# One encoder block on one core: another plan for the mixer jobs, 512-column steps in half of the output projection, one operation fewer in the last chain

## The chip, the core and the metric

The kernel runs on one core of one Trainium2 chip, in one launch. The metric is the device time of that launch in microseconds (us); less is better. Before the change it is 907.31 us, the median of 3 runs (906.53 to 909.83).

## The reference, cut to what matters

One layer of a bidirectional encoder on 512 tokens of width 1024, all in float32:

```python
h = rmsnorm(x, norm1_w)
proj = h @ w_in                                  # 1024 -> 6176 columns
q, k, v, z, xbc, dt_f, dt_b = split(proj)
q, k = partial_rope(q), partial_rope(k)          # 16 heads of 64
attn = dilated_attention(q, k, v)                # three dilated windows, mixed by their denominators
ssm = ssm_mixer(z, xbc, dt_f, dt_b, ...)         # conv + SiLU, two scans (forward, backward), gate, group norm
x = x + concat([attn, ssm]) @ w_out              # 2048 -> 1024
h = rmsnorm(x, norm2_w)
u = dwconv_centered(h @ w_up, ...)               # 1024 -> 5632
x = x + (silu(u[:, :2816]) * u[:, 2816:]) @ w_down
return rmsnorm(x, final_norm_w)
```

## The kernel before

**Products.** Every float32 operand is split into a high and a low part, and each product is three matmuls: high by high, high by low, low by high. A weight tile arrives as `raw` by DMA; ACT copies its high part (`whi`), DVE or POOL subtracts to get the low part (`wlo`) (function `unit`). The free size of a matmul is 512 columns in most jobs, 256 in the jobs that compute v and z and in the output projection, and 128 in transposes.

**Stages.** (1) Warm-up matmuls, the normalised and transposed input `H`, and the first jobs (v0, z0, the step sizes dt). (2) The mixers: some 50 jobs. q0 to q7 and k0 to k7 are the projections of two heads each with rope, v0 to v3 the values, a0 to a7 the attention of two heads; b, c, x, z 0 to 3 are the projections of the state-space mixer with its convolution, s0 to s3 its states, o0 to o3 its output. (3) The output projection, `out_quarter` called for four quarters of 256 columns: 16 row blocks k, four token tiles t, three matmuls each. After a quarter the result is added to x, squared for the norm, transposed and split into `x2w`. (4) 44 up-projection jobs of 24 matmuls, 512 wide. (5) The down projection in two halves of 512 columns; in the second half the last k of each token tile are done tile by tile (`LAST = 4`), tile 3 in two parts of 256 columns, and each tile is normalised and stored as it ends.

**What sets the order.** `weave` takes the next step of the job with the smallest due time. The table `PLAN` gives each job a begin and an end, and the due times run evenly between them. The result is a program order; `list_schedule` then rebuilds the order of every engine with estimated durations (`cost`) and latencies (`LAG`), and that order is written into the program as dependencies. Each engine executes its list strictly in order: an instruction that waits holds up all that stand behind it on its engine.

**Two chains that matter later.** The rope of a q or k job (`rope_rows`, `prep_q`): ACT copies the job's result to `wkp`, DVE shuffles it into a second `wkp`, POOL and DVE multiply by tables (`rpt`), POOL adds, ACT copies the high part to `Q` or `K`, and DVE (or POOL) subtracts for the low part:

```python
        put("Qh", Q[0], qr)
        on("Ql").tensor_sub(lo, qr, f(Q[0]))
```

A b job (`ssm_b`): the convolution is three DVE steps on `B` with an ACT tanh before the third, and PE then transposes B into `trp`. An o job (`ssm_out`) runs per chunk a scan over 1024 elements on DVE (`D`), then sums and products on `D`.

**The last chain.** For each token tile: DVE adds the residual, ACT squares with a sum, DVE adds that sum to the earlier ones (`s3`), DVE scales and adds epsilon (`rs_m`, in `rstd`), POOL raises to the power -1/2, ACT and DVE scale the two halves, SyncE stores them.

Of the kernel before, what the change touches and what calls it, by code (L numbers as in the profile page):

```python
# [10 lines left out]
AF = mybir.ActivationFunctionType  # L11
# [3 lines left out]
SEQ = 512  # L15
DM = 1024
LAST = 4
HEAT = (5, 8)
ROUNDS = 4


PLAN = {"q0": (-60.6, 76), "b0": (-50.4, -31.8), "c1": (-32.3, 72.2), "s0": (-20.3, -2.1), "k1": (-12.3, 6),
# [292 lines left out]
def block_kernel(ctx: ExitStack, tc: tile.TileContext, log, x, w_in, w_out, w_up, w_down,  # L315
# [82 lines left out]
    def PS(tag):  # L398
        return T(tag)

    def SM(shape, tag, bufs=4):
        uid[0] += 1
        return sm.tile(list(shape), F32, name=f"{tag}_{uid[0]}", tag=tag, bufs=bufs)
# [69 lines left out]
            out += [(hi[:, j], lo[:, j]) for j in range(h)]  # L473
        return out

    def job_T(kind, w, c0, rhs, tag="acc"):

        wp = unit(kind, w[:, c0:c0 + 128].rearrange("(k p) c -> p k c", p=128), 8, 128)
        acc = PS(tag)
        n = len(rhs)  # L480
        for k, (rh, rl) in enumerate(rhs):
            hi, lo = wp[k]
            PE.matmul(acc, hi, rh, start=(k == 0), stop=False)
            PE.matmul(acc, hi, rl, start=False, stop=False)
            PE.matmul(acc, lo, rh, start=False, stop=(k == n - 1))
        return acc

    def tok_units(kind, w, c0, tags=("whi", "wlo"), cut=None):
# [565 lines left out]
        SP.dma_start(m, src[(k % 8) * 128:(k % 8 + 1) * 128, :])  # L1054
        split_mix(k, [m], tag)

    def out_quarter(qr, korder, banks):

        c0 = qr * 256
        wo = {}  # L1060
        for n, k in enumerate(korder):
            if k not in wo:
                k0 = k // 4 * 4
                for i, w in enumerate(unit("o", w_out[k0 * 128:(k0 + 4) * 128, c0:c0 + 256]
                                           .rearrange("(k p) c -> p k c", p=128), 4, 256)):
                    wo[k0 + i] = w
# [3 lines left out]
            for t in range(NQ):  # L1070
                o = banks[t // 2][:, (t % 2) * 256:(t % 2 + 1) * 256]
                ts = slice(t * 128, (t + 1) * 128)

                one = PE.matmul(o, mh[:, ts], hi, start=(n == 0 and t % 2 == 0), stop=False).ins
                if n == 0 and t % 2:
                    tc.add_manual_dep(one, opened.name, ISSUE_ORDER, reason="one start opens the bank")
                opened = one
                PE.matmul(o, mh[:, ts], lo, start=False, stop=False)
                PE.matmul(o, ml[:, ts], hi, start=False, stop=(n == 15 and t % 2 == 1))

    obanks = [("acc", "acc"), ("s", "o"), ("E", "y"), ("tr", "trp")]
    first = (0, 1, 2, 3, 8, 9, 10, 11, 4, 5, 12, 13, 6, 14, 15, 7)
    b0 = [PS(tg) for tg in obanks[0]]
    for k in out_quarter(0, first, b0):
# [10 lines left out]
    x2w = []  # L1095
    ss2 = SM([128, 16], "ss2", 1)
    for qr in range(4):
        hf = qr // 2
        if qr == 0:
            banks = b0  # L1100
        else:
            banks = [PS(tg) for tg in obanks[qr]]
            for k in out_quarter(qr, (12, 13, 14, 15, 5, 6, 7, 4, 0, 1, 2, 3, 8, 9, 10, 11), banks):
                if k not in parts:
                    load_mix(k, "hl2")
        cs = slice((qr % 2) * 256, (qr % 2 + 1) * 256)
        for t in range(NQ):
            if qr % 2 == 0:
# [3 lines left out]
            DVE.tensor_add(xx, xx, banks[t // 2][:, (t % 2) * 256:(t % 2 + 1) * 256])  # L1112
            scr = T("fk")
            ACT.activation(scr[:, 0:256], xx, AF.Square, accum_out=ss2[:, 4 * t + qr:4 * t + qr + 1])
        for k in (2 * qr, 2 * qr + 1):
            b = PS("acc" if qr < 3 else ("E", "y")[k % 2])
# [5 lines left out]
            x2w.append((hh, hl))  # L1122
    s2 = SM([128, 4], "s2", 1)
    DVE.tensor_reduce(s2, ss2.rearrange("p (t e) -> p t e", e=4), axis=mybir.AxisListType.X, op=ALU.add)
    r2 = rstd(s2, DM)
    b = PS("o")
    for t in range(NQ):
# [9 lines left out]
    ptags = ["acc", "s", "acc", "tr"]  # L1137

    def up_job(i, j):
        acc = job_T("u", w_up, i * 128, x2w, tag=ptags[j % 4])  # L1140
        u = T("fk")
        DVE.tensor_mul(u, acc, r2b)
        y = T("fk")
        ident_act(y, u, scale=col(P_FW, 3 * i + 1), bias=col(P_FB, i))
        DVE.scalar_tensor_tensor(y[:, 1:512], u[:, 0:511], col(P_FW, 3 * i), y[:, 1:512],
                                 op0=ALU.mult, op1=ALU.add)
        DVE.scalar_tensor_tensor(y[:, 0:511], u[:, 1:512], col(P_FW, 3 * i + 2), y[:, 0:511],
                                 op0=ALU.mult, op1=ALU.add)
        return y
# [12 lines left out]
    fw = [T("fk") for _ in range(2)]  # L1162
    ss3 = SM([128, 16], "ss3", 1)
    nss = [0] * NQ
    for hf in range(2):
        SP.dma_start(fw[hf], bass.AP(tensor=fnorm.tensor, offset=fnorm.offset + hf * 512,
                                          ap=[[0, 128], [1, 512]]))
    for hf in range(2):
# [13 lines left out]
        for k, t, cs in order:  # L1182
            gh, gl = gT[k]
            hi, lo = wd[k]
            ts = slice(t * 128, (t + 1) * 128)
            o = bank[t, cs.start][:, 0:cs.stop - cs.start]
            PE.matmul(o, gh[:, ts], hi[:, cs], start=(k == 0), stop=False)
            PE.matmul(o, gh[:, ts], lo[:, cs], start=False, stop=False)
            PE.matmul(o, gl[:, ts], hi[:, cs], start=False, stop=(k == 21))
            if k < 21:  # L1190
                continue
            n = nss[t]
            nss[t] += 1
            xx = x2[t][hf][:, cs]
            DVE.tensor_add(xx, xx, o)
            scr = T("fk")
            ACT.activation(scr[:, cs], xx, AF.Square, accum_out=ss3[:, 4 * t + n:4 * t + n + 1])
            if hf == 0:
                on("fx").tensor_mul(xx, xx, fw[0])
                continue  # L1200
            if cs.stop < 512:
                DVE.tensor_add(ss3[:, 4 * t:4 * t + 1], ss3[:, 4 * t:4 * t + 1], ss3[:, 4 * t + n:4 * t + n + 1])
                continue
            s3 = SM([128, 1], "s3", 4)
            DVE.tensor_add(s3, ss3[:, 4 * t:4 * t + 1], ss3[:, 4 * t + n:4 * t + n + 1])
# [75 lines left out]
```

## Time and profile before

| | |
|---|---|
| median of 3 runs | 907.31 us |
| the profiled execution: its own time | 908.54 us |
| its span, first to last instruction | 906.8 us |
| mean granted TensorE clock | 0.995 |
| busy PE (matmul) | 887.8 us, 98% |
| busy PEld (weight load, beside PE) | 777.1 us, 86% |
| busy DVE | 613.3 us, 68% |
| busy ACT | 467.2 us, 52% |
| busy POOL | 209.2 us, 23% |

Time in the profile is counted from the first instruction. The profiled execution took 1.74 us more than its span, and 1.23 us more than the median of the runs. All four engines run at once; the share of an engine is an average over stages. Line 142 stands for every instruction, since all are issued through one helper, so groups are told apart by the names of their tiles. The mixers reach from about 60 to 475 us, the output projection from about 440 to 540 us beside their end, the up projection to 780, the down projection to 900, and the rest is the last chain.

### The profile page before, as it was taken

What the parts mean: (1) busy time and instruction counts of PE and PEld (TensorE: products, weight loads), DVE (VectorE), ACT (ScalarE), POOL (GpSimd) and SP (SyncE); (2) the same over time, 40 slices, a digit from 0 to 9 for tenths busy, and PEclk for the clock granted to TensorE, in tenths of its full rate; (3) what the DMA queues carried; (4) which work ended last, traced back from release to release, by engine and by line L of the source; (5) the groups of instructions that cost most, each with busy time, mean ns of one, the idle gap of its engine ahead of it and who ended that gap; (6) DMA issues with size and microseconds to landing.
All of it is one profiled execution on the core that took longest, in us unless ns stands there. A gap on an engine that the chain in (4) does not pass through costs nothing.

```text
span 906.8 us, 13520 instructions
## 1 busy us (share of the span) xinstructions
PE 887.8 (98%) x5084; PEld 777.1 (86%) x5084; DVE 613.3 (68%) x1042; ACT 467.2 (52%) x971; POOL 209.2 (23%) x187
## 2 busy tenths in 40 slices
PE   8989999999999999998999999999999999999997
PEld 7968888999799889997899998888888888888886
DVE  5764879975998787888732337777777777623323
ACT  6454578656575765667843434444444444322222
POOL 1063543422542541364244210000000000000000
PEclk9999999999999999999999999999999999999999
DMA  8465332542444643226474324333333333332312
GB/s 257 140 149 138 89 99 93 163 123 70 113 121 117 173 118 99 70 82 200 132 227 157 94 71 116 94 93 93 98 107 98 93 105 105 96 108 75 116 48 93
DMA packets 123986, 105.07 MB, mean 116 GB/s; under 512 B 5776, under 2 KB 101904, under 8 KB 123920
## 3 DMA queue, kind: packets, MB, share of 16 engines
q1 hardware_dynamic: 123920, 104.20, 39.5%
q8 instruction: 40, 0.66, 0.3%
q14 instruction: 26, 0.21, 0.1%
HBM read 88.91 MB, written 5.83 MB: 104 GB/s over the span
## 4 chain that ended last, share of the span: by engine, by line
PE 88%; DVE 4%; POOL 3%; issue 2%; DMA 1%; ACT 1%; SPq 0%; POOLq 0%; ACTq 0%; DVEq 0%
PE acc L142 44%; PE tr L142 13%; PE s L142 12%; PE o L142 6%; PE y L142 5%; PE E L142 4%; PE trp L142 3%; POOL wkp L142 1%; DVE D L142 1%; POOL wlo L142 1%; DMA raw<-in_w_in_dram 1%; DMA mx<-mixA_d 1%; POOL yy L142 0%; DVE wkp L142 0%; DVE yy L142 0%
## 5 line engine op out<-in xcount | busy, mean ns | idle before, releaser
L142 ACT ACTIVATE whi<-raw 128x512 fp32r<-128x512 f32 x256 | 159.8, 630 | 266.0 <-PE acc L142 135.6
L142 DVE TENSOR_TENSOR wlo<-raw,whi 128x512 fp32r<-128x512 f32 x196 | 140.8, 722 | 99.7 <-ACT whi L142 98.7
L142 PE MATMUL acc<-H,whi 128*128 128x512 f32 x512 | 169.9, 403 | 0.0
L142 POOL TENSOR_TENSOR rs_r<-rs_m,half 128x1 f32<-128x1 f32 (+1 forms) x25 | 16.6, 665 | 425.2 <-DVE rs_m L142 425.2
L142 POOL TENSOR_TENSOR wlo<-raw,whi 128x512 fp32r<-128x512 f32 x60 | 81.4, 1362 | 141.8 <-ACT whi L142 123.6
L142 PEld LDWEIGHTS acc<-H,whi 128*128 128x128 f32 x512 | 94.7, 189 | 17.4
L142 PE MATMUL acc<-x2w,whi 128*128 128x512 f32 x352 | 109.1, 390 | 0.0
L142 PE MATMUL acc<-H,wlo 128*128 128x512 f32 x256 | 102.0, 399 | 0.0
L142 PE MATMUL acc<-whi,H 128*128 128x256 f32 x448 | 87.8, 288 | 2.2 <-ACT H L142 1.8
L142 PEld LDWEIGHTS acc<-x2w,whi 128*128 128x128 f32 x352 | 66.0, 188 | 13.6
L142 DVE SCALAR_TENSOR_TENSOR fk<-fk,prm,fk 128x511 f32<-128x511 f32 x88 | 66.1, 751 | 14.1 <-ACT fk L142 12.6
L142 PEld LDWEIGHTS acc<-whi,H 128*128 128x128 f32 x448 | 72.2, 192 | 3.5 <-ACT H L142 2.1
L142 PE MATMUL acc<-x2w,wlo 128*128 128x512 f32 x176 | 68.6, 390 | 0.0
L142 PE MATMUL acc<-wlo,H 128*128 128x256 f32 x224 | 64.6, 288 | 0.0
L142 DVE TENSOR_TENSOR PT<-tr,PT 128x512 fp32r<-128x512 f32 x64 | 43.7, 683 | 20.7 <-ACT PT L142 20.3
L142 PEld LDWEIGHTS acc<-H,wlo 128*128 128x128 f32 x256 | 48.4, 189 | 9.0
L142 PE MATMUL o<-PT,V 128*128 128x256 f32 x256 | 54.5, 296 | 0.9 <-DVE rs_m L142 0.5
L142 ACT ACTIVATE PT<-tr 128x512 fp32r<-128x512 f32 x64 | 38.1, 596 | 33.0 <-PE tr L142 32.5
L142 PE MATMUL s<-x2w,whi 128*128 128x512 f32 x176 | 54.2, 389 | 0.0
L142 PE MATMUL tr<-x2w,whi 128*128 128x512 f32 x176 | 54.2, 389 | 0.0
L142 DVE CUSTOM_DVE_ANT_0 P<-s,lmx 128x512 f32<-128x512 f32 x64 | 43.8, 684 | 13.7 <-PE s L142 11.4
L142 ACT ACTIVATE P<-P,mn 128x512 f32<-128x512 f32 x64 | 46.0, 718 | 13.0 <-DVE mn L142 12.6
(265 smaller groups left out, 2002.7 us busy)
## 6 DMA issues: line engine op xcount, KB each, us to landing
raw<-in_w_in_dram SPq DMA_DIRECT2D x48, 512.0 KB, 3.9
raw<-in_w_up_dram SPq DMA_DIRECT2D x44, 512.0 KB, 3.7
raw<-in_w_down_dram SPq DMA_DIRECT2D x22, 512.0 KB, 3.6
A<-step_d SPq DMA_DIRECT2D x16, 512.0 KB, 5.4
raw<-in_w_out_dram SPq DMA_DIRECT2D x16, 512.0 KB, 3.4
K<-K SPq DMA_DIRECT2D x48, 128.0 KB, 2.5
mx<-mixA_d SPq DMA_DIRECT2D x13, 256.0 KB, 3.5
mx<-mixS_d SPq DMA_DIRECT2D x10, 256.0 KB, 2.6
```

Source lines behind the costliest of these rows:

```text
L142: r = fn(*args, **kw)
```

## The change

It has three parts. The table `PLAN` gets new numbers, and so every engine gets a new order. The output projection has three parts instead of four quarters: columns 0 to 255, then columns 512 to 1023 at a free size of 512 with one PSUM bank per token tile (`s`, `o`, `E`, `y`), its last two k done tile by tile (`LAST_OUT = 2`), then columns 256 to 511; the up jobs take their k in the order 0, 1, 4, 5, 6, 7, 2, 3. In the last chain the earlier sums are scaled ahead (`sofar`), and one operation (`m3`) takes the place of two.

```diff
+LAST_OUT = 2
...
-PLAN = {"q0": (-60.6, 76), "b0": (-50.4, -31.8), "c1": (-32.3, 72.2), "s0": (-20.3, -2.1), "k1": (-12.3, 6),
...
+PLAN = {"b0": (-82.3, -47.8), "q0": (-78.6, 44.6), "s0": (-32, 26.5), "c1": (-23.8, 67.5), "q2": (-21, 75.6),
...
-    def out_quarter(qr, korder, banks):
+    def out_part(c0, w, korder, banks, last=0):
...
+            for t in range(NQ):
+                if n < 16 - last:
+                    out_step(t, u, w, banks, [k], wo, n == 0, n == 15)
+        for t in range(NQ if last else 0):
+            out_step(t, u, w, banks, korder[16 - last:], wo, False, True)
...
-    obanks = [("acc", "acc"), ("s", "o"), ("E", "y"), ("tr", "trp")]
...
-    for qr in range(4):
...
+    for n, (c0, w, tags, ttags) in enumerate(((0, 256, (), "acc"), (512, 512, ("s", "o", "E", "y"), "acc"),
+                                              (256, 256, ("tr", "trp"), ("E", "y")))):
...
-        acc = job_T("u", w_up, i * 128, x2w, tag=ptags[j % 4])
+        acc = job_T("u", w_up, i * 128, x2w, tag=ptags[j % 4], ks=(0, 1, 4, 5, 6, 7, 2, 3))
...
+            if hf and cs.stop == 512:
+                sofar[t] = SM([128, 1], "sofar", 4)
+                DVE.tensor_scalar(sofar[t], ss3[:, 4 * t:4 * t + 1], 1.0 / DM, EPS, op0=ALU.mult, op1=ALU.add)
...
-            s3 = SM([128, 1], "s3", 4)
-            DVE.tensor_add(s3, ss3[:, 4 * t:4 * t + 1], ss3[:, 4 * t + n:4 * t + n + 1])
-            r3 = rstd(s3, DM)
+
+            s3 = sofar[t]
+            m3, r3 = SM([128, 1], "m3", 4), SM([128, 1], "r3", 4)
+            DVE.scalar_tensor_tensor(m3, ss3[:, 4 * t + n:4 * t + n + 1], 1.0 / DM, s3, op0=ALU.mult, op1=ALU.add)
+            POOL.tensor_tensor(r3, m3, half[:, 0:1], ALU.pow)
```

The counts that follow from it: matmuls of 256 columns 1972 before and 1588 now, of 512 columns 2443 and 2635; POOL 178 tensor operations and 289 DMAs in both.

Place one, the first state-space outputs: DVE's order, before. `wkp_665` is the last step of q0's rope, `B_706` the convolution of b0, `D` the two 1024-element scans of o0's first chunks.

```order
L142 STREAM_SHUFFLE wkp_658<-acc_631 128x512
L142 TENSOR_TENSOR wkp_658<-wkp_658,rpt 128x512
L142 SCALAR_TENSOR_TENSOR D_1353<-A_1352,D_1353 128x1024
L142 TENSOR_TENSOR wkp_665<-wkp_656,Q_663 128x512
L142 SCALAR_TENSOR_TENSOR B_706<-acc_681,hcw,B_706 128x511
L142 TENSOR_TENSOR D_1353<-D_1353 128x512
L142 SCALAR_TENSOR_TENSOR B_706<-acc_681,hcw,B_706 128x511
L142 SCALAR_TENSOR_TENSOR D_1399<-A_1398,D_1399 128x1024
L142 SCALAR_TENSOR_TENSOR B_706<-acc_681,B_706 128x512
```

The same place of DVE now, where b0 is `B_656` and q0's last step is `wkp_713`:

```order
L142 SCALAR_TENSOR_TENSOR B_656<-acc_631,hcw,B_656 128x511 x2
L142 SCALAR_TENSOR_TENSOR B_656<-acc_631,B_656 128x512
L142 SCALAR_TENSOR_TENSOR D_1299<-A_1298,D_1299 128x1024
L142 STREAM_SHUFFLE wkp_706<-acc_679 128x512
L142 TENSOR_TENSOR D_1299<-D_1299 128x512
L142 TENSOR_TENSOR wkp_706<-wkp_706,rpt 128x512
L142 SCALAR_TENSOR_TENSOR D_1345<-A_1344,D_1345 128x1024
L142 TENSOR_TENSOR D_1345<-D_1345 128x512
L142 TENSOR_TENSOR wkp_713<-wkp_704,Q_711 128x512
```

The b0 job now comes before q0, so its three steps stand ahead of both scans and of q0's rope. On PE, the transposes of B moved as well; a piece of the difference (`trp_712` before, `trp_662` now; the matmuls `s` are a0's first):

```order
 L142 MATMUL acc_729<-H_103,wlo_726 128x512
-L142 MATMUL trp_712<-ident,B_706 128x128 x4
 L142 MATMUL acc_783<-H_101,whi_775 128x512
...
 L142 MATMUL acc_906<-H_103,wlo_903 128x512
-L142 MATMUL s_940<-K_761,Q_663 128x512
-L142 MATMUL s_940<-K_762,Q_663 128x512
-L142 MATMUL trp_981<-ident,xs_890 128x128
+L142 MATMUL s_983<-K_761,Q_711 128x512
+L142 MATMUL s_983<-K_762,Q_711 128x512
+L142 MATMUL trp_662<-ident,B_656 128x128 x4
 L142 MATMUL acc_1076<-H_101,whi_1068 128x512
```

Before, the transposes stood behind the first job after b0's own (job k1, `acc_729`); now they stand four jobs later.

Place two, near the end of the mixers: DVE's order, before. `wkp_4695` is the last rope step of job q7, `P` and `mn` the softmax of a6 and a7, `yy` and `rs_m` the gate and norm of o3.

```order
L142 ISA mn_4771 128x1
L142 TENSOR_TENSOR yy_4733<-yy_4733,zs_4121 128x256
L142 TENSOR_TENSOR wkp_4695<-wkp_4686,Q_4693 128x512
L142 TENSOR_TENSOR D_5172<-D_5172,CM_4136 128x512
L142 TENSOR_TENSOR wlo_5228<-raw_5221,whi_5227 128x512
L142 TENSOR_SCALAR rs_m_4742<-ssS_4740 128x1
L142 ISA P_4803,mn_4804<-s_4800,lmx 128x512
```

The same place of DVE now (q7's last rope step is `wkp_4553`):

```order
L142 TENSOR_TENSOR m_4203<-wkp_4506,o_4387 64x512
L142 TENSOR_TENSOR V_4637<-acc_4579,V_4637 128x2x64
L142 TENSOR_TENSOR wkp_4553<-wkp_4544,Q_4551 128x512
L142 ISA P_4770,mn_4771<-s_4767,lmx 128x512
L142 ISA mn_4771 128x1
L142 TENSOR_SCALAR yy_4452<-yy_4452,rs_r_4463 128x256
L142 TENSOR_TENSOR wk_4731<-E_4728,ein 128x512
L142 TENSOR_TENSOR m_4203<-m_4203,tr_4750 128x512
L142 ISA P_4803,mn_4804<-s_4800,lmx 128x512
```

q7's last rope step stood between the softmax rows `mn_4771` and `P_4803`; it now stands ahead of `P_4770`, and the v3 job's rows (`V`) have come into this place.

Place three, the end: ACT's order, before. `x_1365` and `x_1270` are the two halves of token tile 2, `x_1367` and `x_1272` those of tile 3; `fk, ss` is a square with its sum.

```order
L142 ACTIVATE fk_9250,ss_1810_8405<-x_1365_6157 128x512
L142 ACTIVATE fk_9275,ss_1810_8405<-x_1367_6162 128x256
L142 ACTIVATE x_1270_5567<-x_1270_5567,rs_r_9256 128x512
L142 ACTIVATE fk_9291,ss_1810_8405<-x_1367_6162 128x256
L142 ACTIVATE x_1272_5572<-x_1272_5572,rs_r_9297 128x512
```

The end of ACT's order now (tile 2 is `x_1355`, tile 3 `x_1357`):

```order
L142 ACTIVATE fk_9071,ss_1806_8201<-x_1357_5940 128x256
L142 ACTIVATE fk_9048,ss_1806_8201<-x_1355_5935 128x512
L142 ACTIVATE x_1270_5567<-x_1270_5567,r_1941_9051 128x512
L142 ACTIVATE fk_9089,ss_1806_8201<-x_1357_5940 128x256
L142 ACTIVATE x_1272_5572<-x_1272_5572,r_1946_9092 128x512
```

Tile 3's first square now comes before tile 2's. On PE the last 512-wide matmuls of tile 2 were followed by 24 matmuls of 256 columns; now 18 of 256 columns follow them.

## Rows read from the trace of the kernel before

**Rows 1.** Stretch 396 to 480 us: length, busy PE, PEld, DVE, ACT, POOL, clock, DMA, GB/s.

```profile
396.00:480.00 84.00, 79.56 (x569) 72.57 (x568) 58.08 (x112) 56.87 (x128) 38.09 (x31) 1.00 0.54 168
```

**Rows 2.** Chain that ended last: start us, us, engine and tile, count; three widths.

```profile
478.45 0.72 PE o L142 x6
...
542.44 0.44 PE o L142 x4
...
545.41 5.44 PE s L142 x24
```

**Rows 3.** PE's waits, 0:66, 66:396 and 396:480 us: total us, times, longest.

```profile
PE trp L142 <- DVE B L142: 3.5, 1, 3.5
...
PE y L142 <- DVE xd L142: 0.6, 1, 0.6
...
PE tr L142 <- DVE PT L142: 1.3, 2, 0.8
PE tr L142 <- ACT wkp L142: 0.7, 1, 0.7
PE o L142 <- DVE rs_m L142: 0.5, 1, 0.5
...
PE o L142 <- ACT PT L142: 0.4, 1, 0.4
PE s L142 <- DVE mn L142: 0.3, 1, 0.3
```

**Rows 4.** Timeline of DVE, 58 to 66 us; in brackets idle before, releaser.

```profile
58.45 1.10 DVE L142 TENSOR_TENSOR wkp<-wkp,Q 128x512 fp32r<-128x512 f32 x1 [1.79 <-ACT Q L142]
...
61.18 0.74 DVE L142 SCALAR_TENSOR_TENSOR B<-acc,hcw,B 128x511 f32<-128x511 f32 x1
61.84 2.70 DVE L142 TENSOR_TENSOR_SCAN D<-A,D 128x1024 f32<-128x1024 f32 x1
64.46 0.66 DVE L142 SCALAR_TENSOR_TENSOR B<-acc,B 128x512 f32<-128x512 f32 x1
...
65.68 1.70 DVE L142 TENSOR_TENSOR D<-D 128x512 f32<-128x512 f32 x1
```

**Rows 5.** Timelines of POOL, ACT and DVE, 402 to 412 us: q7's rope.

```profile
402.50 4.68 POOL L142 TENSOR_TENSOR wlo<-raw,whi 128x512 fp32r<-128x512 f32 x3
407.14 1.30 POOL L142 TENSOR_TENSOR wkp<-wkp,rpt 128x512 f32<-128x512 f32 x1
...
409.90 0.63 ACT L142 ACTIVATE Q<-wkp 128x512 fp32r<-128x512 f32 x1 [3.73 <-POOL wkp L142]
...
410.56 0.69 DVE L142 TENSOR_TENSOR wkp<-wkp,Q 128x512 fp32r<-128x512 f32 x1 [1.84 <-ACT Q L142]
411.17 0.69 DVE L142 TENSOR_TENSOR D<-D,CM 128x512 f32<-128x512 f32 x1
```

**Rows 6.** Stretch 412.44 to 432.12 us, columns as in rows 1.

```profile
412.44:432.12 19.68, 17.53 (x122) 14.79 (x121) 17.57 (x40) 15.54 (x37) 9.29 (x9) 1.00 0.68 200
```

**Rows 7.** Timelines of DVE and ACT, 897 to 902 us: the last chain.

```profile
897.40 0.69 DVE L142 TENSOR_TENSOR x<-x,tr 128x512 f32<-128x512 f32 x1 [0.46 <-PE tr L142]
...
900.27 0.42 DVE L142 TENSOR_TENSOR x<-x,acc 128x256 f32<-128x256 f32 x1 [0.76 <-PE acc L142]
...
901.34 0.15 DVE L142 TENSOR_TENSOR s<-ss 128x1 f32<-128x1 f32 x1
901.53 0.15 DVE L142 TENSOR_SCALAR rs_m<-s 128x1 f32<-128x1 f32 x1
...
900.18 0.72 ACT L142 ACTIVATE x<-x,rs_r 128x512 f32<-128x512 f32 x1 [0.38 <-POOL rs_r L142]
900.81 0.40 ACT L142 ACTIVATE fk<-x 128x256 f32<-128x256 f32 x1
```

**Rows 8.** Timeline of ACT, 9 to 11 us: the first weights.

```profile
9.85 1.15 ACT L142 ACTIVATE whi<-raw 128x512 fp32r<-128x512 f32 x2 [0.64 <-DMA raw<-in_w_in_dram]
```

More of the change, by code (lines that the diff above doesn't have):

```diff
@@ L474, in unit, with job_T @@
         return out
-    def job_T(kind, w, c0, rhs, tag="acc"):
+    def job_T(kind, w, c0, rhs, tag="acc", ks=range(KO)):
         wp = unit(kind, w[:, c0:c0 + 128].rearrange("(k p) c -> p k c", p=128), 8, 128)
         acc = PS(tag)
-        n = len(rhs)
-        for k, (rh, rl) in enumerate(rhs):
+        for k in ks:
+            rh, rl = rhs[k]
             hi, lo = wp[k]
-            PE.matmul(acc, hi, rh, start=(k == 0), stop=False)
+            PE.matmul(acc, hi, rh, start=(k == ks[0]), stop=False)
             PE.matmul(acc, hi, rl, start=False, stop=False)
-            PE.matmul(acc, lo, rh, start=False, stop=(k == n - 1))
+            PE.matmul(acc, lo, rh, start=False, stop=(k == ks[-1]))
         return acc
@@ L1055, in load_mix @@
         split_mix(k, [m], tag)
-    def out_quarter(qr, korder, banks):
-        c0 = qr * 256
+    def out_part(c0, w, korder, banks, last=0):
         wo = {}
+        u = 512 // w
         for n, k in enumerate(korder):
             if k not in wo:
[L1063 to L1066, printed above, removed]
+                k0 = k // (2 * u) * (2 * u)
+                for i, wk in enumerate(unit("o", w_out[k0 * 128:(k0 + 2 * u) * 128, c0:c0 + w]
+                                            .rearrange("(k p) c -> p k c", p=128), 2 * u, w)):
+                    wo[k0 + i] = wk
@@ L1067, in out_quarter, with out_step @@
             yield k
+            for t in range(NQ):
[3 more added lines that the diff above has]
+            out_step(t, u, w, banks, korder[16 - last:], wo, False, True)
+    def out_step(t, u, w, banks, ks, wo, first, end):
+        o = banks[t // u][:, (t % u) * w:(t % u + 1) * w]
+        ts = slice(t * 128, (t + 1) * 128)
+        for k in ks:
             mh, ml = parts[k]
             hi, lo = wo[k]
[L1070 to L1079, printed above, removed]
@@ L1081, in block_kernel @@
-    obanks = [("acc", "acc"), ("s", "o"), ("E", "y"), ("tr", "trp")]
+            one = PE.matmul(o, mh[:, ts], hi, start=first and t % u == 0, stop=False).ins
+            if first and t % u:
+                tc.add_manual_dep(one, opened[0].name, ISSUE_ORDER, reason="one start opens the bank")
+            opened[:] = [one]
+            PE.matmul(o, mh[:, ts], lo, start=False, stop=False)
+            PE.matmul(o, ml[:, ts], hi, start=False, stop=end and k == ks[-1] and t % u == u - 1)
+    opened = []
@@ L1082, in block_kernel @@
     first = (0, 1, 2, 3, 8, 9, 10, 11, 4, 5, 12, 13, 6, 14, 15, 7)
-    b0 = [PS(tg) for tg in obanks[0]]
-    for k in out_quarter(0, first, b0):
+    b0 = [PS("acc"), PS("acc")]
+    for k in out_part(0, 256, first, b0):
         if k in (14, 15):
@@ L1094, in block_kernel @@
     x2 = [[None, None] for _ in range(NQ)]
-    x2w = []
-    ss2 = SM([128, 16], "ss2", 1)
-    for qr in range(4):
[L1098 to L1103, printed above, removed]
+    x2w = [None] * KO
+    ss2 = SM([128, 12], "ss2", 1)
+    rest = (12, 13, 14, 15, 5, 6, 7, 4, 0, 1, 2, 3, 8, 9, 10, 11)
+    for n, (c0, w, tags, ttags) in enumerate(((0, 256, (), "acc"), (512, 512, ("s", "o", "E", "y"), "acc"),
+                                              (256, 256, ("tr", "trp"), ("E", "y")))):
+        hf = c0 // 512
+        u = 512 // w
+        banks = b0 if n == 0 else [PS(tg) for tg in tags]
+        if n:
+            for k in out_part(c0, w, rest, banks, LAST_OUT if n == 1 else 0):
                 if k not in parts:
                     load_mix(k, "hl2")
-        cs = slice((qr % 2) * 256, (qr % 2 + 1) * 256)
+        cs = slice(c0 % 512, c0 % 512 + w)
         for t in range(NQ):
-            if qr % 2 == 0:
+            if x2[t][hf] is None:
                 x2[t][hf] = T("x2")
@@ L1111, in block_kernel @@
             xx = x2[t][hf][:, cs]
-            DVE.tensor_add(xx, xx, banks[t // 2][:, (t % 2) * 256:(t % 2 + 1) * 256])
+            DVE.tensor_add(xx, xx, banks[t // u][:, (t % u) * w:(t % u + 1) * w])
             scr = T("fk")
-            ACT.activation(scr[:, 0:256], xx, AF.Square, accum_out=ss2[:, 4 * t + qr:4 * t + qr + 1])
-        for k in (2 * qr, 2 * qr + 1):
-            b = PS("acc" if qr < 3 else ("E", "y")[k % 2])
+            ACT.activation(scr[:, 0:w], xx, AF.Square, accum_out=ss2[:, 3 * t + n:3 * t + n + 1])
+        for k in range(c0 // 128, (c0 + w) // 128):
+            b = PS(ttags if n < 2 else ttags[k % 2])
             for t in range(NQ):
@@ L1121, in block_kernel @@
             DVE.scalar_tensor_tensor(hl, b, col(P_N2, k), f(hh), op0=ALU.mult, op1=ALU.subtract)
-            x2w.append((hh, hl))
+            x2w[k] = (hh, hl)
     s2 = SM([128, 4], "s2", 1)
-    DVE.tensor_reduce(s2, ss2.rearrange("p (t e) -> p t e", e=4), axis=mybir.AxisListType.X, op=ALU.add)
+    DVE.tensor_reduce(s2, ss2.rearrange("p (t e) -> p t e", e=3), axis=mybir.AxisListType.X, op=ALU.add)
     r2 = rstd(s2, DM)
@@ L1164, in block_kernel @@
     nss = [0] * NQ
+    sofar = {}
     for hf in range(2):
```

19 rows, old and new, of the table PLAN are left out of this document.

## The prediction

> **What bounds the kernel now.** I read the shares first: PE is busy 98% of the span at a clock of 0.995, so time can come only from fewer or cheaper columns on PE, from the few places where PE stands still, and from the end, where PE has finished and the last chain runs alone. Then I read PE's pitch, the time from one matmul's start to the next, in pieces of the chain of waits where nothing interrupts: six matmuls of 256 columns in 0.72 us, so 0.120 us each; 24 of 512 in 5.44 us, so 0.2267 each; four transposes in 0.44 us, so 0.11 each [rows 2]. Third, PE's waits: before the mixers' tail only two matter, 3.5 us for tile B and 0.6 us for xd; from 396 to 480 us there are eight which sum to 4.2 us, of which the five that belong to attention and the gate (PT from DVE and ACT, wkp, rs_m, mn) hold 3.2 [rows 3]. In that stretch PE is busy 79.56 of 84.00 us, so 4.44 us idle [rows 1]. The up and down projections show no such gap. Last I read what DVE did ahead of the two worst places.
>
> At the first place DVE waits 1.79 us, in order, for ACT's Q of q0's rope; then come the steps of b0's convolution, and between the second and the third of them a scan of 2.70 us. The third step ends at 65.12 us, and PE has stood 3.5 us for the transposes of B [rows 3, 4]. At the second place POOL works off three wlo (4.68 us) before q7's rope; the rope's result reaches DVE at 410.56 us, after 1.84 us of idleness in order [rows 5], and from there DVE is busy 17.57 of 19.68 us, about as much as PE's 17.53 [rows 6]: two engines at once near their limits, so each delay of one is a wait of the other.
>
> **The change part by part.** The sum is made against the profiled execution, 908.54 us, which is 1.23 above the median.
>
> *512-column steps.* 384 matmuls of 256 columns go and 192 of 512 come, with the same columns in all: 384 x 0.120 - 192 x 0.2267 = 46.08 - 43.53 = 2.55 us less [rows 2], all on PE's path, since this stage keeps PE full except at its start. The steps themselves hide nothing new: weights come in pieces of the same 512 KB, and after a token tile's last matmul six more of 128 columns and six of the next part stand ahead of its transposes (6 x 0.11 + 6 x 0.12 = 1.38 us), more than DVE's add of 0.69 [rows 7]. **-2.55.**
>
> The Trainium skill, page "TensorE: Matmul & The Clock Gate", section "Back-to-back issue gap", gives a matmul alone N/2.4 + 2.5 ns when warm. By that two of 256 would take 218.3 and one of 512 215.8 ns, and 192 such pairs would give back 0.5 us in place of 2.55; the trace's 240 against 226.7 speaks against it, and it is a rival below.
>
> *The first place.* Now b0's three steps stand ahead of both scans and of q0's rope, and PE's transposes of B behind the sixth job after b0's own, not the first. One job is 24 x 0.2267 = 5.44 us [rows 2], so PE has five jobs, 27 us, more of other work, while DVE's list up to the third step got shorter. The wait should vanish: **-3.5**, with 0 at the worst, if something else on DVE's list takes its place there. I take the full amount because what PE needs next (a0's first scores) also stands behind all these jobs.
>
> *The tail.* q7's job starts some 18 us of PE's work earlier, and its last rope step leaves the place between two softmaxes. I counted what each engine has in its list from softmax P_4803 to the last low part that the first output part needs. Before: DVE 17.7 us; PE 65 x 0.12 + 38 x 0.11 + 11 x 0.227 + 4 x 0.19 = 15.3, so DVE was the longer by 2.4. Now: DVE 19.9; PE 70 x 0.12 + 40 x 0.11 + 33 x 0.227 + 8 x 0.19 = 21.8, so PE is the longer by 1.9 (0.19 for o3's products in plain float32, an estimate between the pitches of the two widths; the 18 us above and these counts come from the order at the pitch of rows 2). The five waits of attention and gate should go, those on weights and on the mixers' read-back (1.0 us) stay: **-3.2** [rows 3]. Bounds: 0, if the waits only move, and -4.4, the whole idle time [rows 1].
>
> *xd.* The wait of 0.6 us [rows 3] hangs on a rope whose order changes little: 0, at best -0.6.
>
> *New waits.* The new order sets ropes elsewhere. For each q and k job I counted PE's work from the job's end to the first instruction that needs what DVE has behind the rope, against ACT's copy, POOL's 1.30 us steps, ACT's 0.63 and DVE's rows [rows 5]. Before, three places came out negative, among them the two that PE stood at. Now none does; the thinnest have 0.4 and 0.5 us left (k7's rope, and the one before a1's scores), the next 1.5 and 2.1. A rope that comes late holds DVE 1.8 us (1.79 and 1.84 in the two cases seen [rows 4, 5]). I take **+0.5**, between 0 and 3.6 for the two thinnest.
>
> *The last chain.* One DVE operation goes, and its step is 0.19 us (901.34 to 901.53 [rows 7]). But look at what holds the chain: the last 256 columns were added from 900.27 on, yet ACT's square of them starts at 900.81, since ACT first scales tile 2 (900.18, in order) [rows 7]. Tile 2's add began at 897.40, right after its last matmul, with 24 matmuls of 256 columns behind it; now 18 follow, so tile 2 ends 6 x 0.12 = 0.72 us nearer to the end. Its own chain (add 0.69, square, one operation fewer, power, scale) takes about 2.3 us up to ACT's scale; counted on, ACT comes to the last square about 0.2 us later than before. The two cancel: **0**, between -0.2 and +0.2.
>
> *The start.* All 13 warm-up matmuls now come in one go, and SyncE issues four x tiles ahead of the parameters. The first real job waits for its weights, which land at 9.85 us [rows 8] and keep their place in the queue: 0; one copy of 0.6 us (half of that row's two) later at the worst.
>
> **Sum:** -2.55 - 3.5 - 3.2 + 0.5 = -8.75. The profiled execution would take 899.8 us, the median **898.6 us**.
>
> **The rivals.**
>
> *The waits move* (same). The tail keeps two engines near their limit: 19.9 us of DVE's work against 21.8 is no wide margin, and my counts put all DVE rows end to end. If the tail's 3.2 us come back elsewhere and one or both thin ropes turn into a wait of 1.8, the sum is -2.55 - 3.5 + 1.8 = -4.25 or + 3.6 = -2.45: 903.1 to 904.9 us. For it speaks that three wlo in a row took POOL 4.68 us, so that a rope can be late for reasons outside its own list [rows 5]; against it, that q7's rope, the worst, has moved away.
>
> *POOL falls behind* (slower). One mechanism: POOL and DVE slow each other. The same add on D took 1.70 us at 65.68 and a product on it 0.69 at 411.17 [rows 4, 5]. If the new order sets POOL's steps beside DVE's two-input steps more often, POOL's ropes come late everywhere; it decides from about 2.1 us of lateness, where all four thin places (0.4, 0.5, 1.5, 2.1) stop PE. At the price of the first place, 3.5 us each, that is +14.0 against -2.55 - 3.5 - 3.2: +4.75, 912.1 us. Against it: the counts of POOL's work did not change, and it is busy 23% of the span.
>
> The Trainium skill, page "SBUF — State Buffer", section "Who interferes with whom", says that a DVE instruction with two SBUF inputs contends with a GpSimd instruction that reads SBUF; the 1.70 us agree, and by it the second rival depends on pairings that the order doesn't tell.
>
> *Width brings nothing.* If two narrow matmuls cost what one wide one does but for 0.5 us in all, the sum is -0.5 - 3.5 - 3.2 + 0.5 = -6.7: 900.6 us. The 240 against 226.7 ns of the rows are plain, so this is small.
>
> *All idle time goes.* Tail at -4.4, xd at -0.6, no new waits, chain at -0.2: -11.25, so 896.1 us; with the spread of the runs (the fastest was 0.8 below the median) 895.3, and a little more if short gaps hide inside PE's busy time.
>
> **How the numbers follow.** Forecast 0.66, width brings nothing 0.08, all idle time goes 0.04, the waits move 0.18, POOL falls behind 0.04. A measurement of this kernel can tell about 0.5%, 4.5 us, from no change, so the border is 902.8 us: faster 0.66 + 0.08 + 0.04 = 0.78, same 0.18, slower 0.04. The range is 894.8 to 904.5: down to the case in which all idle time goes, and up to nearly both thin ropes late; outside are the slower rival and the edges of the others.
>
> **What would show it.** In the profile of the changed kernel: no wait of PE for B near 60 us (right), or a wait of 2 us or more for Q, K, P or PT within the next 30 us (moved). In the tail, PE's idle time from 396 to 480 us below 1.5 us instead of 4.44, and DVE's waits for ACT's Q below 1 us. In the output projection a pitch of 0.227 us on s, o, E, y with the transposes following without a gap; 0.24 would say that width brings nothing. At the end, the time from the last matmul to the last instruction within 0.2 us of 6.5 (900.27 [rows 7] to the span's 906.8). The prediction is wrong if a single wait of over 2 us stands anywhere between 60 and 480 us, or if the first place's wait is gone and the span fell by less than 5 us.

## The result, and the profile after

The changed kernel takes 899.03 us (median of 4 runs, 898.54 to 900.22), the kernel before 907.75 us in the same comparison (4 runs, 906.53 to 909.83). The ratio is 0.990, with a 95% interval of 0.988 to 0.993, so about 8.7 us less by the medians. Run again beside the last experiments it came out at 0.990 (0.988 to 0.993). The forecast was 898.6 us, and the time lies in the stated range. Its terms are another matter: the largest one came out at less than a third of its size, and another was too small by 0.9 us.

The profiled execution took 898.54 us with a span of 896.7 us. The difference of the two spans, 10.1 us, is larger than that of the medians, because the profiled execution of before (908.54) lies above its median and that of the changed kernel is the shortest of its four.

First the stretches in which the two places lay, with busy time by engine, in the changed kernel. The columns are those of [rows 1]: start and end, length, then busy PE, PEld, DVE, ACT, POOL with their counts, the granted clock, the DMA share and GB/s.

```profile
50.00:80.00 30.00, 27.57 (x115) 22.34 (x114) 22.37 (x24) 12.52 (x24) 21.42 (x12) 0.94 0.77 180
...
396.00:480.00 84.00, 83.70 (x559) 75.58 (x558) 61.22 (x115) 57.80 (x130) 40.02 (x32) 1.00 0.53 166
```

From 396 to 480 us PE's idle time fell from 4.44 us [rows 1] to 84.00 - 83.70 = 0.30. From 50 to 80 us it is 2.43 us. The same row of the kernel before says that it was 3.49 there:

```profile
50.00:80.00 30.00, 26.51 (x114) 21.66 (x113) 17.49 (x19) 12.77 (x26) 22.17 (x14) 0.94 0.73 176
```

So the tail gave more than expected and the first place much less. From 80 to 396 us PE is idle for some 0.7 us in both.

PE's waits in the changed kernel, from 66 to 396 and from 396 to 480 us, answer to [rows 3]:

```profile
PE acc L142 <- DVE wkp L142: 2.4, 1, 2.4
PE trp L142 <- ACT yy L142: 0.5, 1, 0.5
PE tr L142 <- DVE PT L142: 0.2, 1, 0.2
...
PE s L142 <- DVE mn L142: 0.2, 1, 0.2
```

The wait for B is gone, but a wait of 2.4 us stands in its place, and it is paid twice like the one for B: behind it the granted clock is low, and only nine matmuls ran in 3.55 us.

```profile
68.20:72.00 3.80, 3.55 (x9) 2.77 (x10) 3.08 (x4) 0.61 (x1) 3.80 (x3) 0.57 0.68 196
```

The view names what the wait is for: PE cannot begin the next job because its bank (`acc`) has not yet been read by DVE's shuffle into `wkp`. The waits of the tail, eight lines with 4.2 us in all, have come down to one of 0.2; the wait for xd is gone. One wait is new at the start of the kernel, where SyncE now issues four x tiles ahead of the parameters:

```profile
PE E L142 <- DMA prm<-in_params_dram: 1.9, 1, 1.9
```

It stands in all nine profiles with the new table, at 0.4 to 2.0 us, and in none of the five with the old one.

What holds that shuffle? The timeline of DVE at this place, to be compared with [rows 4]:

```profile
53.43 2.28 DVE L142 TENSOR_TENSOR_SCAN D<-A,D 128x1024 f32<-128x1024 f32 x1
...
59.04 3.38 DVE L142 TENSOR_TENSOR_SCAN D<-A,D 128x1024 f32<-128x1024 f32 x1
62.45 1.60 DVE L142 TENSOR_TENSOR D<-D 128x512 f32<-128x512 f32 x1
65.89 1.10 DVE L142 TENSOR_TENSOR wkp<-wkp,Q 128x512 fp32r<-128x512 f32 x1 [1.84 <-ACT Q L142]
67.66 0.01 DVE L142 LOAD_MASK_SELECT wkp<-acc  x1 [0.67 <-ACT wkp L142]
67.66 0.73 DVE L142 STREAM_SHUFFLE wkp<-acc 128x512 f32<-128x512 f32 x1
```

then that of POOL in the same stretch, and two rows of ACT:

```profile
53.42 5.15 POOL L142 TENSOR_TENSOR wlo<-raw,whi 128x512 fp32r<-128x512 f32 x2 [1.01 <-ACT whi L142]
58.54 1.73 POOL L142 TENSOR_TENSOR wkp<-wkp,rpt 128x512 f32<-128x512 f32 x1
60.23 3.27 POOL L142 TENSOR_TENSOR wlo<-raw,whi 128x512 fp32r<-128x512 f32 x1
63.46 1.74 POOL L142 TENSOR_TENSOR wkp<-wkp,wkp 128x512 f32<-128x512 f32 x1
...
65.23 0.63 ACT L142 ACTIVATE Q<-wkp 128x512 fp32r<-128x512 f32 x1 [4.14 <-POOL wkp L142]
...
67.03 0.60 ACT L142 ACTIVATE wkp<-acc 128x512 f32<-128x512 f32 x1 [0.64 <-DVE wkp L142]
```

Read from below: the shuffle waits for ACT's copy of the next rope, that copy stands behind q0's last step (its `wkp` buffer comes free then), that step waits 1.84 us for ACT's Q, and Q waits for POOL's add, which ends at 65.2 us. The same rope as before [rows 4] is late again, only other work is queued behind it. POOL's lateness is not the whole of the 2.4 us: DVE's own scan and sum end only at 64.05 us, so with a faster POOL q0's last step could have begun at most 1.84 us earlier.

The same add was slow in the kernel before already; this row of its trace was there to be read:

```profile
54.47 3.28 POOL L142 TENSOR_TENSOR wkp<-wkp,wkp 128x512 f32<-128x512 f32 x1
```

The 512-wide steps in the chain that ended last, answering to [rows 2]:

```profile
490.86 0.68 PE o L142 x3
491.54 0.68 PE E L142 x3
```

Three matmuls in 0.68 us, 0.227 each, and no gap. The end, from the timelines of DVE and ACT, answers to [rows 7]:

```profile
890.29 0.42 DVE L142 TENSOR_TENSOR x<-x,acc 128x256 f32<-128x256 f32 x1 [0.52 <-PE acc L142]
...
892.41 0.75 DVE L142 SCALAR_TENSOR_TENSOR x<-x,r,fk 128x512 f32<-128x512 f32 x1 [0.66 <-POOL r L142]
...
890.44 0.72 ACT L142 ACTIVATE x<-x,r 128x512 f32<-128x512 f32 x1 [0.85 <-POOL r L142]
891.07 0.40 ACT L142 ACTIVATE fk<-x 128x256 f32<-128x256 f32 x1
```

From the start of the last add to ACT's last square it is now 0.78 us, where it was 0.54 [rows 7]. From the same start to the last instruction it is 896.7 - 890.29 = 6.41 us, where it was 6.53.

### The profile page after: what moved, and what is told of

Same layout as the page of the kernel before. It is cut to its first block, busy times and chain, and to the rows that moved or that the text cites. A ratio compares the mean times of both kernels' runs of the same rounds, so it can differ in the third digit from the quotient of the medians.

```text
span 896.7 us, 13139 instructions
## 1 busy us (share of the span) xinstructions
PE 881.9 (98%) x4892; PEld 764.9 (85%) x4892; DVE 617.0 (69%) x1038; ACT 463.5 (52%) x963; POOL 220.4 (25%) x187
## 4 chain that ended last, share of the span: by engine, by line
PE 53%; DMA 1%; DVE 0%; ACT 0%; issue 0%; POOLq 0%; POOL 0%; SPq 0%; DVEq 0%; ACTq 0%
PE acc L142 20%; PE tr L142 11%; PE s L142 10%; PE o L142 4%; PE E L142 3%; PE y L142 3%; PE trp L142 2%; DMA mx<-mixA_d 1%; DMA mixA_d<-m 0%; DVE m L142 0%; DVE x L142 0%; ACT fk L142 0%; ACT hl L142 0%; ACT wkp L142 0%; POOLq L1284 0%
## 5 line engine op out<-in xcount | busy, mean ns | idle before, releaser
L142 POOL TENSOR_TENSOR wlo<-raw,whi 128x512 fp32r<-128x512 f32 x60 | 91.5, 1531 | 131.2 <-ACT whi L142 126.1
L142 POOL TENSOR_TENSOR r<-m,half 128x1 f32<-128x1 f32 x4 | 2.2, 548 | 359.2 <-DVE m L142 359.2
```

Of the source, the lines that this page charges most:

```text
L142: r = fn(*args, **kw)
```

## The experiments

The theory after the result: the parts add up; the tail's waits began with q7's late rope; the first place was traded for a second wait of the same origin, q0's rope late on POOL; the chain's saving was cancelled. Where a kernel below moves one instruction in the finished order, it does so with a helper that takes the instructions that use certain tiles and sets them behind another (shown as in the later runs; the earlier ones have no `first`):

```diff
+def place(queue, log, moved, behind, last=0, first=None):
+    def has(i, names):
+        return all(any(t == n or t.startswith(n + "_") for t in log.tiles[i]) for n in names)
+    take = [i for i in queue if has(i, moved)][-last:][:first]
+    rest = [i for i in queue if i not in take]
+    at = max(n for n, i in enumerate(rest) if has(i, behind)) + 1
+    queue[:] = rest[:at] + take + rest[at:]
```

### The parts alone

The kernel before with the new table and nothing else:

```diff
-PLAN = {"q0": (-60.6, 76), "b0": (-50.4, -31.8), ...
+PLAN = {"b0": (-82.3, -47.8), "q0": (-78.6, 44.6), ...
```

> Only the table of job times is new. If the parts add up: the whole change gave 8.7 us and 192 wide matmuls for 384 narrow ones are worth 2.5, so this should take 6.2 us less than before (901.5 us), with PE idle below 1.5 us from 396 to 480 us and the 2.4 us wait of PE for a rope's shuffle near 66 us in place of the wait for B. Rival, the tail was eased by the wide steps and not by the plan: only 2 to 3 us less, and 3 us or more of idle PE from 396 to 480 us.

Measured: ratio 0.993 (0.992 to 0.995) to a median of 908.33, so 6.1 us less (7.0 by the medians). Its row for the tail:

```profile
396.00:480.00 84.00, 83.27 (x635) 78.87 (x634) 56.64 (x108) 57.21 (x127) 36.02 (x32) 1.00 0.55 175
```

PE's idle time is 0.73 us, and its waits name the same 2.4 us for `wkp`. The plan alone does what it does in the whole change; the rival falls.

The changed output projection with the old table and the old last chain:

```diff
-    for qr in range(4):
+    for n, (c0, w, tags, ttags) in enumerate(((0, 256, (), "acc"), (512, 512, ("s", "o", "E", "y"), "acc"),
+                                              (256, 256, ("tr", "trp"), ("E", "y")))):
```

> Only the output projection is new, with the old table of job times and the old last chain. If width is worth its pitch: 2.5 us less than before (905.2 us), the wait of 3.5 us for B and the idle 4.4 us from 396 to 480 us as they were. Rival, width brings nothing: 0.5 us less at most, with a pitch of 0.24 us on banks s, o, E, y. Rival, the new list also eases the tail: 5 us less.

Measured: ratio 0.9985 (0.997 to 1.000), 1.4 us less, with -2.5 and -0.2 as the ends of the interval (2.3 us less by the medians). The wait for B is 3.5 us as before; the pitch, in the chain that ended last, is that of the changed kernel:

```profile
485.06 0.68 PE s L143 x3
```

The stretch of the tail:

```profile
396.00:480.00 84.00, 80.48 (x533) 71.03 (x532) 60.74 (x117) 57.63 (x132) 39.90 (x32) 1.00 0.55 169
```

The tail is idle for 3.52 us instead of 4.44, so this part eased it by 0.92 us, where none of that was expected. That the wide steps cost 0.227 us each is shown, so 192 of them take 2.55 us less than 384 of 0.120; that the whole of it reaches the time is only compatible with the interval's end. In the one profile of this run, 5.29 us lie between the last scaling and the last instruction, where it is 4.28 to 4.48 in all the others; whether its other executions have this too was not seen. The two parts together (-6.1 and -1.4) make 7.5 of the 8.7, or 9.3 by the medians, which is within their intervals.

The kernel before with the shorter last chain alone:

```diff
+            DVE.scalar_tensor_tensor(m3, ss3[:, 4 * t + n:4 * t + n + 1], 1.0 / DM, s3, op0=ALU.mult, op1=ALU.add)
-            DVE.tensor_add(s3, ss3[:, 4 * t:4 * t + 1], ss3[:, 4 * t + n:4 * t + n + 1])
-            r3 = rstd(s3, DM)
```

> Only the last chain is new. As I read it, the operation saved (0.19 us) is given back because tile 2 now ends nearer to the end and ACT scales it before the last square: 6.5 us from the start of the last add to the last instruction, as before, within 0.1. Rival, the saving arrives: 6.3 us.

Measured in one run (909.40 us), in the timeline of DVE:

```profile
901.13 0.42 DVE L142 TENSOR_TENSOR x<-x,acc 128x256 f32<-128x256 f32 x1 [0.50 <-PE acc L142]
...
903.28 0.75 DVE L142 SCALAR_TENSOR_TENSOR x<-x,r,fk 128x512 f32<-128x512 f32 x1 [0.66 <-POOL r L142]
```

From the last add to the last instruction (span 907.6) it is 6.47 us, where before it was 906.8 - 900.27 = 6.53; from the add to the last scaling 2.15 where it was 2.17. The saving is gone, as expected. The counter-test is the changed kernel with the old order at the end:

```diff
+    place(pe, log, ("trp_1873",), ("tr_1872",), 12)
+    place(act, log, ("fk_1942",), ("fk_1939",))
+    place(dve, log, ("x2_1357", "trp_1873"), ("x2_1355", "tr_1872"))
```

> The changed kernel, with tile 2 finished ahead of tile 3's first 256 columns at the end, as before the change, on PE, DVE and ACT. If the shorter chain was cancelled by tile 2's later end: 0.2 us less from the start of the last add to the last instruction than in the changed kernel (6.3 for 6.5). Rival, the order at the end doesn't matter: no difference.

Measured in one run (897.93 us):

```profile
889.92 0.42 DVE L142 TENSOR_TENSOR x<-x,acc 128x256 f32<-128x256 f32 x1 [0.74 <-PE acc L142]
...
891.82 0.75 DVE L142 SCALAR_TENSOR_TENSOR x<-x,r,fk 128x512 f32<-128x512 f32 x1 [0.66 <-POOL r L142]
```

1.90 us from the add to the scaling instead of 892.41 - 890.29 = 2.12, and 896.1 - 889.92 = 6.18 us from the add to the last instruction instead of 6.41, both 0.2 us less: the operation saved is worth its 0.2 us as soon as tile 2 ends where it did. The scheduler, not the edit, had taken it back. The step repeats: it is 1.90 us in the other run with the old end (below, with both moves at q0's rope), and 2.12 or 2.13 in five other runs with the new one.

### The tail: q7's place

The kernel before, with two numbers of the table changed:

```diff
-        "o3": (311.2, 440.8), "q7": (319.8, 332.9), "a6": (327.7, 378)}
+        "o3": (311.2, 440.8), "q7": (286.4, 341.9), "a6": (327.7, 378)}
```

> The kernel before, with job q7's begin and end alone moved to the values of the new table. If q7's late rope starts the waits of the tail: idle PE from 396 to 480 us falls from 4.4 to about 1.5 us, and the time by 3 us (904.5 us). Rival, DVE is simply the longer engine there, and the plan as a whole moved work into the tail for PE: less than 1 us gained, idle PE stays above 3 us.

Measured: ratio 0.997 (0.9955 to 0.9987), 2.6 us less (1.2 to 4.1). The stretch of the tail:

```profile
396.00:480.00 84.00, 82.23 (x622) 77.12 (x620) 57.67 (x114) 57.32 (x129) 34.46 (x29) 1.00 0.54 169
```

PE is idle for 1.77 us instead of 4.44. The other way round, the changed kernel with q7 back at its old place:

```diff
-        "a4": (264.8, 269.3), "k6": (266.7, 341.9), "x3": (275.7, 282.9), "z3": (280.7, 281.2), "q7": (286.4, 341.9),
+        "a4": (264.8, 269.3), "k6": (266.7, 341.9), "x3": (275.7, 282.9), "z3": (280.7, 281.2), "q7": (319.8, 332.9),
```

> The changed kernel, with job q7 alone moved back to its old begin and end. If its late rope starts the waits of the tail: idle PE from 396 to 480 us rises by about 3 us, and the time by 3 us (902 us). Rival, the rest of the plan eased the tail: it rises by less than 1 us.

Measured: ratio to before 0.992 (0.9905 to 0.993), where the changed kernel had 0.990: some 1.5 us more, and the intervals overlap. The same stretch:

```profile
396.00:480.00 84.00, 81.48 (x531) 71.95 (x530) 59.92 (x116) 56.63 (x129) 40.60 (x33) 1.00 0.53 168
```

Idle PE went from 0.30 to 2.52 us, of which one wait of 1.3 us (`tr` for DVE's m) is more than half. So q7's two numbers account for 2.7 of the 4.1 us of idle time removed, counted from before, or 2.2, counted from after. The remaining 1.4 to 1.9 are shared by the rest of the plan and the wide steps (0.92 alone), which no run takes apart.

That the late rope itself carries these waits is not shown. The two numbers change more than q7's place: in the first of these kernels the order of instructions differs from that of before in many places from about 311 us on. And with q7 back at its old place, DVE did not wait for q7's rope, but for another step of POOL:

```profile
408.99 0.87 DVE L142 TENSOR_TENSOR wkp<-wkp,Q 128x512 fp32r<-128x512 f32 x1
...
412.32 0.42 DVE L142 TENSOR_TENSOR yy<-yy,y 128x256 f32<-128x256 f32 x1 [1.44 <-POOL yy L142]
```

The product `m` behind that step is the one for which PE waited 1.3 us.

### The first place

The kernel before, with the third step of b0's convolution ahead of the scan that stood between the steps:

```diff
+    place(dve, log, ("A_288", "D_289"), ("B_122", "acc_121"))
```

> The kernel before; in DVE's list alone, the third step of b0's convolution moves ahead of the scan of 2.7 us that stood between the second and the third. If that scan made about half of the wait for B: 3.5 falls to about 1.7 us and the time by 1.8 us (905.9 us); the rest is q0's rope, for which DVE waits 1.8 us before. Rival, the rope made all of it: the wait stays at 3 us or more. Rival, the scan made all of it: below 0.5 us.

Measured: ratio 0.9955 (0.994 to 0.997), 4.1 us less (2.8 to 5.3). PE's wait from 50 to 100 us:

```profile
PE trp L142 <- DVE B L142: 1.7, 1, 1.7
```

The stretch from 50 to 80 us:

```profile
50.00:80.00 30.00, 28.29 (x127) 23.02 (x126) 20.53 (x22) 14.04 (x28) 23.52 (x14) 1.00 0.75 184
```

The wait fell to 1.7 us as the theory said, but the time fell by more than twice that. The clock is a part of it: it was 0.94 in this stretch before and is 1.00 here, and PE got through 13 matmuls more, which are 2.9 us at 0.227 each; the shorter wait makes 1.8 of them. In the four runs of this kernel the mean clock was 0.996 or 0.997, in the nine of the kernel before on the same chip 0.990 to 0.995. In the kernel before, after PE had stood 3.5 us, the matmuls that followed ran at about half speed, as a short stretch of its trace shows:

```profile
65.10:68.00 2.90, 2.82 (x9) 2.44 (x10) 2.89 (x4) 0.60 (x1) 1.74 (x2) 0.51 1.07 274
```

A clock of 0.51 is the lower of the two levels, 1.2 GHz for 2.4 (four of the nine matmuls are transposes of 128 columns). So a long wait can be paid twice, and taking away half of it can save all of the second payment; that it is not paid twice in every execution is shown in the last section.

The changed kernel, with POOL's add of q0's rope ahead of one low part:

```diff
+    place(pool, log, ("wlo_153",), ("wkp_120", "wkp_121"))
```

> The changed kernel; in POOL's list alone, the last step of q0's rope (an add) moves ahead of one low part of weights (wlo) that stood before it. If the new wait of 2.4 us near 66 us is q0's rope coming late from POOL, and DVE, which holds the next shuffle and with it PE's bank, waiting in order: the wait is gone or below 0.4 us, and with it the eight half-speed matmuls behind it, 2.5 to 4 us less than the changed kernel (895 to 896.5 us). Rival, the scan of 3.4 us on DVE holds the shuffle: at least 1.5 us of the wait stays.

Measured: ratio to before 0.988 (0.987 to 0.9895), against the changed kernel's 0.990, so perhaps 2 us less; 898.34 us beside 909.24 on its chip. It is the fastest version by its ratio, but its interval overlaps that of the changed kernel, and on the same chip the changed kernel with only its end reordered took 897.93 us in its one run. So a gain over the changed kernel is not shown. PE's waits from 50 to 82 us:

```profile
PE acc L142 <- DVE wkp L142: 1.2, 1, 1.2
PE acc L142 <- DVE C L142: 1.1, 1, 1.1
```

Neither theory had this. The wait for the shuffle halved, a new one of 1.1 us appeared at the convolution of c (DVE had waited in order for the next rope), and the sum is hardly smaller; the clock, though, stayed at 1.00 through both. POOL and DVE show why the move brought only half:

```profile
60.77 1.73 POOL L142 TENSOR_TENSOR wkp<-wkp,rpt 128x512 f32<-128x512 f32 x1
62.58 3.15 POOL L142 TENSOR_TENSOR wkp<-wkp,wkp 128x512 f32<-128x512 f32 x1
...
64.69 1.60 DVE L142 TENSOR_TENSOR D<-D 128x512 f32<-128x512 f32 x1
66.43 1.55 DVE L142 TENSOR_TENSOR wkp<-wkp,Q 128x512 fp32r<-128x512 f32 x1
```

The add now runs beside DVE's scan and takes 3.15 us instead of 1.74. But a faster add would have helped by 0.14 us at most: DVE's own scan and sum end at 66.29 us, and q0's last step begins at 66.43. So the rival is half right too: the scan on DVE holds the shuffle as much as POOL does. The next runs take the scan away, first alone:

```diff
+    place(dve, log, ("D_277",), ("wkp_132", "rpt"), 0, 2)
```

> The changed kernel; in DVE's list alone, the second scan of o0 and the sum behind it move behind q0's last rope step and the next rope's first two. Theory: the scan beside POOL makes POOL's rope steps and low parts slow (3.15 to 3.3 us for what takes 1.28 alone), and this is why q0's rope is late. Then the add ends some 2 us earlier and the wait of 2.4 us near 66 us is below 0.5 us: 3 us less than the changed kernel (896 us). Rival, only the order of POOL's list counts, and DVE does not slow it: the wait stays above 1 us.

Measured: ratio 0.993 (0.991 to 0.995), slower than the changed kernel by about 3 us. The theory was right on POOL and wrong on the time. POOL, with no scan beside it:

```profile
62.32 1.28 POOL L142 TENSOR_TENSOR wlo<-raw,whi 128x512 fp32r<-128x512 f32 x1
63.58 1.28 POOL L142 TENSOR_TENSOR wkp<-wkp,wkp 128x512 f32<-128x512 f32 x1
```

1.28 us for what took 3.27 and 1.74, and no wait for the shuffle; but the scan and its sum, now ahead of c's convolution, hold PE there:

```profile
PE acc L142 <- DVE C L142: 3.7, 1, 3.7
PE s L142 <- DMA K<-K: 0.7, 1, 0.7
```

With both moves:

```diff
+    place(pool, log, ("wlo_153",), ("wkp_120", "wkp_121"))
+    place(dve, log, ("D_277",), ("wkp_132", "rpt"), 0, 2)
```

> As the run with the scan moved, and q0's add ahead of one low part on POOL as well. With both, the two waits of 1.2 and 1.1 us that the POOL move alone left near 68 and 75 us are gone or sum to less than 0.5 us: 3 to 4 us less than the changed kernel. Rival, the wait moves on to the next conv or rope job: 1 us or more remains between 60 and 90 us.

Measured: ratio 0.9915 (0.9895 to 0.9935), 900.0 us: the rival holds. Two waits remain:

```profile
PE acc L142 <- DVE C L142: 2.9, 1, 2.9
PE s L142 <- DMA K<-K: 2.2, 1, 2.2
```

With the old order at the end as well:

```diff
...
+    place(pe, log, ("trp_1873",), ("tr_1872",), 12)
+    place(act, log, ("fk_1942",), ("fk_1939",))
+    place(dve, log, ("x2_1357", "trp_1873"), ("x2_1355", "tr_1872"))
```

> Both moves at q0's rope, and tile 2 finished ahead of tile 3 at the end: the sum of the parts, 0.2 us less than with the two moves alone, 895 to 896 us, faster than both kernels. Rival: no more than the POOL move alone gave, about 898.

Measured: ratio 0.9925 (0.990 to 0.995), 901.0 us, not told apart from the run before it and not the 895 expected. In this stretch DVE has two scans, two ropes and three convolutions to do; at both places of the second scan that were tried, PE waited behind it for one thing or another. Where it would fit without a wait was not found.

The changed kernel on the same chip:

> The changed kernel once more, on the chip of these runs, so that they are compared with it directly: 0.990 of the kernel before.

Measured: 898.75 us beside 908.3, ratio 0.990 (0.988 to 0.993), as the first time.

## Why the prediction was right, and where it was not

The total, -8.75 us predicted and -8.7 measured, is right, for reasons that are in part wrong: that they agree to 0.1 us is luck, as the terms below show.

- **512-column steps, -2.55.** The pitch came out as forecast, three matmuls in 0.68 us. The part alone moved the time by 1.4 us with -2.5 as one end of the interval, so the term may be a little high. (The traces have 2020 and 1636 matmuls of 256 columns, 48 more in both than the counts given under the change; the difference, 384, is the same.) That width brings nothing fell with the pitch. The Trainium skill's formula for a matmul alone, page "TensorE: Matmul & The Clock Gate", section "Back-to-back issue gap", which the prediction quotes, does not describe this stream: it gives 215.8 ns for 512 columns, and 226.7 were measured.
- **The first place, -3.5.** This step failed. "The wait should vanish" held for B, and I had priced "something else on DVE's list takes its place there" at the worst end and not taken it. The idle time from 50 to 80 us fell by 1.06 us, not 3.5. The reason given, that what PE needs next are a0's first scores, looked at data alone: what PE needed first was its bank `acc`, which DVE's next shuffle had not read yet. And the count of rope margins took POOL's steps at 1.30 us, end to end. Around q0's rope five POOL operations ran beside DVE's scans, sums and products and took 5.15 + 1.73 + 3.27 + 1.74 = 11.9 us instead of 6.5, and DVE's second scan and sum took 3.38 + 1.60 us where 2.28 and 0.68 are the shortest in the same trace. The row of before, 3.28 us for this very add, would have warned. With the scan moved away the last low part and the add on POOL took 1.28 us each and the wait for the shuffle was gone, so the scan at this place is shown as the cause; of its two effects, POOL's lateness makes at most 1.84 of the 2.4 us, and the rest is DVE's own time. The sum also has no term for the clock, which a long wait can cost on top.
- **The tail, -3.2.** Too small in size: idle time fell by 4.14 us, near the bound of 4.4. That the waits go is right; moving q7's job made the largest part (2.2 to 2.7 us of idle time), but that its late rope was what held the others is only argued. That the waits on weights and read-back "stay" was wrong; they went with the rest.
- **xd, 0.** Its 0.6 us went, and 0.5 us for another transpose (`trp` for ACT's yy) came.
- **New waits, +0.5.** At the two places named as thin (k7's rope, and the one before a1's scores) there was none; the one that came, 2.4 us, stood at a rope that was not named.
- **The last chain, 0.** Right, and shown from both sides: 6.47 for 6.53 us with the chain alone, and 0.2 us back when tile 2 ends earlier.
- **The start, 0.** PE's idle time in the first 50 us was 3.83 us before and 4.90 and 4.35 in two profiles of the changed kernel, while the five profiles with the old table lie between 3.76 and 4.28 and the nine with the new one between 3.30 and 4.90: not told apart. Not foreseen was PE's wait for the parameters, which now come behind four x tiles; a wait for ACT's H, 1.3 to 2.3 us with the old table, is down to 0.6 us or less.

So the first place fell short by 2.4 us; the tail gave 0.9 more, and the 0.5 kept for new waits is in the first place's 2.43 us already. By these corrections the sum would be -8.75 + 2.4 - 0.9 - 0.5 = -7.75, a microsecond short of the measured one, which its interval (-6.8 to -10.7) does not tell apart. By its own test ("a single wait of over 2 us anywhere between 60 and 480 us") the prediction's account was wrong at the first place, whatever the sum.

The rival that POOL falls behind named the right mechanism, POOL and DVE slowing each other, but as an event at four places at once; it happened at one, at which the price was a wait of 2.4 us in place of one of 3.5.

## What to carry to other kernels

A margin in an ordered list has to be counted with durations from the neighbourhood in which the step will run: where POOL works beside two-input work on DVE, its rows there are the price, not its rows elsewhere. When a wait is taken away, ask which later instruction the same late chain holds up, a buffer that is not yet read as well as data that is not yet there. Moving one row took 4.1 us off the kernel before, but in the changed kernel, around q0's rope, it only moved the wait. And a shorter chain should be looked at in the new order, since the scheduler may end another tile later and take the saving back.

## What the runs showed of the hardware

**A scan and POOL slow each other.** DVE's scan of 1024 elements took 2.28 us at best and 3.38 beside a rope step and a low part on POOL; POOL's add of 512 took 1.28 us alone and 3.15 beside the scan. Which of the two is slowed differs: the changed kernel's first scan took its 2.28 us beside two low parts of POOL, and only these were slow (5.15 us for two). I had expected something of the kind, but not a factor of 2.5. The Trainium skill, page "SBUF — State Buffer", section "Who interferes with whom", says that a DVE instruction with two SBUF inputs contends with a GpSimd instruction that reads SBUF; the rows agree and give the size for this pair.

**The same wait is not always paid twice.** The kernel before, the run with the chain alone and the run with q7 early all have the wait of 3.5 us for B, and up to 300 us the same order of instructions. The row of before from 50 to 80 us stands above; this is the row of the run with the chain alone:

```profile
50.00:80.00 30.00, 26.51 (x109) 21.56 (x108) 16.64 (x18) 12.54 (x25) 21.29 (x14) 0.89 0.74 174
```

and with q7 early:

```profile
50.00:80.00 30.00, 26.51 (x119) 21.70 (x118) 20.13 (x22) 13.80 (x27) 22.16 (x14) 1.00 0.74 179
```

All three were busy for 26.51 of 30 us, but at a clock of 0.94, 0.89 and 1.00 they got through 114, 109 and 119 matmuls. Ten matmuls, at most 0.227 us each, are up to 2.3 us: that much one long wait of PE adds or does not add, from one profiled execution to another. The wait of 2.4 us is no different: the clock from 50 to 80 us was 0.94 in the changed kernel and 1.00 in the run with the new table alone. In one kernel, too, the time goes with the clock, here over the whole run: on one chip the kernel before took 905.43 us at a mean clock of 0.999 and 910.99 us at 0.993.
